# A two-layer hybrid trunk: the bias table loaded ready-made, transposes grouped, norm operations metered, boundary and last stage re-timed

## The chip, the cores and the metric

One core of one Trainium2 chip runs the whole kernel. The metric is device time in microseconds, the median of three runs. Its engines are TensorE (PE; PEld is its weight load), VectorE (DVE), ScalarE (ACT), GpSimd (POOL) and SyncE (SP), whose queue issues most DMA transfers.

## The reference

The input x is 256 x 2048 in float32. Each of two layers computes:

```
h    = rmsnorm(x, pre_g)
q,k,v,z_att,u,z_ssm = split(h @ w_in)            # 2048 x 6144
w    = softmax(q1 k1/8 + bias, mask) - lam * softmax(q2 k2/8 + bias, mask)   # 8 heads
att  = rmsnorm(w @ v, subln_g) * (1 - lam_init) * silu(z_att)
y    = Re(C h_state) + D u     # diagonal complex state space, 64 groups
ssm  = glu(gelu(y) @ w_glu) * silu(z_ssm)
x    = x + rmsnorm([att, ssm] @ w_out, post_g)
```

The bias is the T5 table: `table[bucket(key - query), head]`, the same for both layers. It depends on key minus query alone, so one row of 383 values per head says all of it.

## The kernel before

**Weights in two parts.** Every weight matrix is cut into half chunks of 128 x 1024, 288 in all (144 per layer). SP loads each into a `raw` tile, ScalarE rounds it to `hi` (`emit_hi`, L220), VectorE forms `lo` = raw - hi (`emit_lo`, L238). The activations have two parts as well (`hthi`, `htlo`). `main` (L1018) multiplies hi x hi, hi x lo and lo x hi, so a half chunk is 24 matmuls of 256 columns or 12 of 512. `emit_hi` and `emit_lo` run two half chunks ahead of `main`, SP six.

**Order within a layer** (half chunk numbers s): U4 and u, the state-space input (0 to 15), q and k (16 to 47), v and z_att (48 to 79), z_ssm (80 to 95), glu (96 to 111), out (112 to 143).

**Side work.** Everything else is written as generators, started by `hooks` (L1127) at a given s. In each half chunk `run_first` (L296) advances those that don't want TensorE, then come `emit_lo` and `main`, and `run_second` (L302) advances those that yielded a number, which is how many PSUM `side` buffers they want (four in all). So a `yield` is half a chunk's time. VectorE operations of long chains stand in two queues: `weave` (parameters, scan) and `urgent` (norms). `fill` (L206) takes from them before and after each `lo`, up to a budget in ns by the costs of `cost` (L126). The budget is a balance, `bal` (L1283), which gains 2880 ns (s < 48) or 2724 ns per half chunk, less `SPARE` and the work already issued. With `urgent` operations present the budget is `UB` = 1500 instead, and `fill` takes one from each queue in turn.

**Steps that the change touches.** `load_params` and `params_gen` (L319, L329) make the bias: a one-hot matrix times the table on TensorE (`psp`), a copy on ScalarE, a store to `tab`, a broadcast to `tabs`, and a load with a shifted address into `bias`. `rstd_gen` (L627) makes 1/rms of x; its last step is the matmul `psr` and the copy `rbc`, which the evacuations of U4 and u (`evac`, L950) need. `newton_ops` (L260) is an inverse square root by two steps. `prep_gen` (L470) clears `cm` on GpSimd and turns the state-space matrices into `wi` through transposes `psw`. `attfin_gen` (L932) scales and transposes one head of attention. `y_gen` (L795) makes the state-space output: matmuls `psy` and `psz`, GELU, transposes `psg`. At the boundary (L1229 to L1265) and at the end (L1295 to L1302) `rowend` (L1100) takes the norm of the out product for rows 0 to 127 (t = 0) and 128 to 255 (t = 1), `late_mg` (L1108) multiplies its last quarter by the norm weight, `add_ops` (L1112) adds x. `warm` (L1181) issues matmuls whose result nobody reads; `build` (L607) transposes x for the new layer (`psx`).

Of the kernel before, what the change touches and what calls it, by code (L numbers as in the profile page):

```python
# [39 lines left out]
W3 = 4  # L40
WB = 1
# [7 lines left out]
TPS = ([(0, 1024), (1024, 1024)], [(0, 512), (512, 768), (1280, 768)])  # L49
WY = 2  # L50
UB = 1500
# [35 lines left out]
def hybrid_trunk(ctx: ExitStack, tc, x, rel_bias, post_norm_g, xt_in, wst, vecs, poles, lams, bc, onehot, out):  # L87
# [57 lines left out]
    def mul(o, a, b):  # L145
        return tt(o, a, b, ALU.mult)
# [31 lines left out]
    tabs = dp.tile([128, 3072], F32, name="tabs")  # L178
    tab = dp.tile([8, 384], F32, name="tab")
# [26 lines left out]
    def fill(budget, force=False):  # L206
        while (budget > 0 and weave) or (urgent and (force or budget > 0)):
            if urgent:
                try:
                    budget -= next(urgent[0])  # L210
                except StopIteration:
                    urgent.popleft()
            if not weave or budget <= 0:
                continue
            try:
                budget -= next(weave[0])
            except StopIteration:
                weave.popleft()
# [19 lines left out]
    def emit_lo(hs, budget, halves=False, parts=(0, 1)):  # L238
# [6 lines left out]
        if (weave and budget > 0) or urgent:  # L245
            budget = UB if urgent else budget
# [13 lines left out]
    def newton_ops(o, v, n, i=0):  # L260
# [3 lines left out]
        yield ts(y.bitcast(I32), v.bitcast(I32), -0.5, float(0x5F380000), ALU.mult, ALU.add)  # L264
        yield mul(h, y, y)
# [53 lines left out]
    def load_params():  # L319
# [4 lines left out]
        G.dma_start(out=bt[0:32, 0:384], in_=onehot)  # L324
        G.dma_start(out=bt[0:32, 384:392], in_=rel_bias)
# [3 lines left out]
    def params_gen():  # L329
# [3 lines left out]
        yield 2  # L333
        ps = side("psp")
        mm4(ps[0:8, 0:320], bt[0:32, 384:392], bt[0:32, 0:320], True, True)
        ps2 = side("psp2")
        mm4(ps2[0:8, 0:64], bt[0:32, 384:392], bt[0:32, 320:384], True, True)
# [7 lines left out]
        act(bt[0:8, 1024:1344], ps[0:8, 0:320], AF.Copy)  # L345
        act(bt[0:8, 1344:1408], ps2[0:8, 0:64], AF.Copy)
        weave.append(params_ops(T, bt))
        SY.dma_start(out=tab, in_=bt[0:8, 1024:1408])
# [9 lines left out]
        SY.dma_start(out=tabs, in_=tab.rearrange("h r -> (h r)").unsqueeze(0).to_broadcast([128, 3072]))  # L358
        for _ in range(8):
            yield  # L360
        SY.dma_start(out=bias, in_=bass.AP(tensor=tabs.tensor, offset=tabs.offset + 127,
                                          ap=[[3071, 128], [384, 8], [1, 256]]))
# [107 lines left out]
    def prep_gen(l, slots):  # L470
# [55 lines left out]
        for b0 in range(0, 8, nb):  # L526
# [80 lines left out]
    def build(l, m):  # L607
# [19 lines left out]
    def rstd_gen(l):  # L627
# [43 lines left out]
        if l == 0:  # L671
            yield
# [46 lines left out]
    def s_gen(l):  # L719
# [6 lines left out]
        for b0 in range(0, 8, 2):  # L726
            if b0 == 4:
                while not (S["u2"] and f"wi{l}" in S):
                    yield
                yield  # L730
# [3 lines left out]
            for b in (b0, b0 + 1):  # L734
                wi = S[f"wi{l}" if b >= 4 else f"wa{l}"][b // 4]
                for h in range(2):
                    for a in range(2):
                        for r, g in ((0, 0), (1, 1), (1, 0), (0, 1)):
                            rows, o = slice(64 * g, 64 * g + 64), 64 * (g ^ r)
                            q, c = 2 * h + r, 256 * a + 64 * (2 * (b - b0) + h)  # L740
                            mm4(pss[r][o:o + 64, c:c + 64], wi[rows, b % 4, 2 * q + a], U[rows, 8 * q + b], True, True)
# [190 lines left out]
    def attfin_gen(l, h):  # L932
        yield from until(f"scal{l}{h // 4}")
        sc = S[f"scal{l}{h // 4}"]
        za = S["za"]
        for t in range(2):
            c = slice(1024 * t + 128 * h, 1024 * t + 128 * h + 128)
            act(za[:, c], za[:, c], AF.Copy, scale=sc[:, 2 * (h % 4) + t:2 * (h % 4) + t + 1])
# [3 lines left out]
        for t in range(2):  # L942
            tpose(ps[:, 128 * t:128 * t + 128], za[:, 1024 * t + 128 * h:1024 * t + 128 * h + 128], ident)
# [430 lines left out]
```

## Time and profile before

| | us |
|---|---|
| median of 3 runs (lowest, highest) | 923.97 (923.2, 924.18) |
| the profiled execution's own time | 924.31 |
| its span, first to last instruction | 922.5 |
| TensorE busy in the span | 901.3 |
| VectorE busy | 674.2 |
| ScalarE busy | 487.1 |
| GpSimd busy | 13.7 |

The mean granted TensorE clock is 0.99 of full speed. TensorE's busy time holds matmuls at either clock, and the matmuls of `warm`. A pause of any other engine costs time only if TensorE, or the end, waits for it.

### The profile page before, as it was taken

The numbers are of one execution on the slowest core, as the hardware profiler recorded it, in microseconds if no ns is written. First come the engines' busy times: TensorE is split into PE (matmuls) and PEld (weight loads), VectorE is DVE, ScalarE is ACT, GpSimd is POOL, SyncE is SP. The second block draws the span as 40 slices with busy tenths as digits, with TensorE's granted clock in tenths as the row PEclk, the third lists the DMA queues.
The fourth block names the chain that finished last, engine by engine and source line by source line (L and its number), as shares of the span: only waits on it lengthen the run. The fifth ranks groups of instructions, "written<-read, shape, count | busy, mean of one in ns | idle before, by whom it ended". The sixth has DMA issues, their size and how long they took to land.

```text
span 922.5 us, 16345 instructions
## 1 busy us (share of the span) xinstructions
PE 901.3 (98%) x6344; PEld 775.3 (84%) x6344; DVE 674.2 (73%) x1202; ACT 487.1 (53%) x878; POOL 13.7 (1%) x19
## 2 busy tenths in 40 slices
PE   9989999999999899999999999999999999999995
PEld 8989999888778688888889888887888888888884
DVE  5978894998975757898677549888966465665564
ACT  6623357465465576444469453445565665644451
POOL 2000000000000000000000000000000000000001
PEclk9999999999999999999999999999999999999998
DMA  8767566755452467567646765865545346665862
GB/s 326 233 190 233 182 218 170 224 176 166 138 183 94 136 224 233 172 226 242 211 152 188 247 209 130 267 198 168 178 137 182 116 138 205 203 208 165 293 181 92
DMA packets 65069, 176.11 MB, mean 191 GB/s; under 512 B 17574, under 2 KB 24512, under 8 KB 64096
## 3 DMA queue, kind: packets, MB, share of 16 engines
q1 hardware_dynamic: 64704, 174.89, 59.9%
q8 instruction: 50, 0.82, 0.4%
q14 instruction: 27, 0.22, 0.1%
q0 software_dynamic: 144, 0.15, 0.1%
q10 hardware_dynamic: 144, 0.03, 0.0%
HBM read 167.42 MB, written 7.88 MB: 190 GB/s over the span
## 4 chain that ended last, share of the span: by engine, by line
PE 86%; DVE 4%; ACT 2%; issue 1%; DVEq 0%; ACTq 0%
PE ac L139 78%; PE lga L139 1%; DVE lo L142 1%; PE psy L139 1%; PE po L139 1%; ACT wi L160 1%; PE pss L139 1%; DVE sct L142 1%; PE acu L139 1%; ACT hi L160 1%; PE pwt L123 1%; PE pst L139 0%; PE psm L123 0%; PE psf L123 0%; DVE nwh L142 0%
## 5 line engine op out<-in xcount | busy, mean ns | idle before, releaser
L160 ACT ACTIVATE hi<-raw 128x1024 fp32r<-128x1024 f32 (+1 forms) x282 | 298.1, 1057 | 358.8 <-PE ac L139 307.7
L142 DVE TENSOR_TENSOR lo<-raw,hi 128x1024 fp32r<-128x1024 f32 (+1 forms) x282 | 343.0, 1218 | 116.5 <-ACT hi L160 113.5
L139 PE MATMUL ac<-ht,hi 128*128 128x256 f32 (+1 forms) x1104 | 257.6, 319 | 3.7 <-DVE u L142 2.5
L139 PE MATMUL ac<-hi,ht 128*128 128x512 f32 x768 | 251.1, 398 | 0.0
L139 PEld LDWEIGHTS ac<-ht,hi 128*128 128x128 f32 x1104 | 184.3, 193 | 18.9 <-issue 2.9
L139 PE MATMUL ac<-ht,lo 128*128 128x256 f32 x704 | 199.3, 284 | 0.4 <-DVE lo L142 0.4
L139 PEld LDWEIGHTS ac<-hi,ht 128*128 128x128 f32 x768 | 144.9, 189 | 31.9
L139 PE MATMUL ac<-lo,ht 128*128 128x512 f32 x384 | 150.8, 393 | 2.1 <-DVE lo L142 2.0
L139 PE MATMUL ac<-hi,mx 128*128 128x512 f32 x456 | 141.8, 390 | 0.0
L139 PEld LDWEIGHTS ac<-ht,lo 128*128 128x128 f32 x704 | 135.2, 192 | 0.9 <-DVE lo L142 0.9
L139 PEld LDWEIGHTS ac<-hi,mx 128*128 128x128 f32 x456 | 85.6, 188 | 17.7
L139 PE MATMUL ac<-lo,mx 128*128 128x512 f32 x228 | 88.7, 389 | 0.0
L139 PEld LDWEIGHTS ac<-lo,ht 128*128 128x128 f32 x384 | 72.6, 189 | 17.5 <-DVE lo L142 3.7
L139 PE MATMUL ac<-hi,ghi 128*128 128x512 f32 x128 | 51.6, 403 | 0.0
L139 PEld LDWEIGHTS ac<-lo,mx 128*128 128x128 f32 x228 | 42.8, 188 | 8.9
L139 PE MATMUL ac<-hi,glo 128*128 128x512 f32 x128 | 50.2, 392 | 0.0
L139 PE MATMUL ac<-lo,ghi 128*128 128x512 f32 x128 | 49.9, 390 | 0.0
L149 DVE SCALAR_TENSOR_TENSOR y<-y 128x512 f32<-128x512 f32 x16 | 11.1, 692 | 28.2 <-ACT y L160 28.0
L160 ACT ACTIVATE att<-att,mx 128x128 f32<-128x128 f32 x64 | 28.4, 446 | 5.4 <-DVE mx L871 5.1
L139 PEld LDWEIGHTS ac<-hi,glo 128*128 128x128 f32 x128 | 24.0, 188 | 5.2
L139 PEld LDWEIGHTS ac<-lo,ghi 128*128 128x128 f32 x128 | 24.1, 188 | 4.6
L139 PEld LDWEIGHTS ac<-hi,ghi 128*128 128x128 f32 x128 | 24.0, 188 | 4.5
(202 smaller groups left out, 964.2 us busy)
## 6 DMA issues: line engine op xcount, KB each, us to landing
raw<-in_wst_dram SPq DMA_DIRECT2D x287, 512.0 KB, 4.0
U<-uds SPq DMA_DIRECT2D x48, 64.0 KB, 3.4
bt<-in_bc_dram SPq DMA_DIRECT2D x4, 512.0 KB, 6.4
uds<-u SPq DMA_DIRECT2D x4, 512.0 KB, 6.0
pg<-in_post_norm_g_dram SPq DMA_DIRECT2D x2, 1024.0 KB, 6.9
xt<-in_x_dram SPq DMA_DIRECT2D x2, 1024.0 KB, 7.4
xt<-xsave SPq DMA_DIRECT2D x2, 1024.0 KB, 6.2
tabs<-tab SPq DMA_DIRECT2D x1, 1536.0 KB, 8.3
```

Source lines behind the costliest of these rows:

```text
L123: P.transpose(o, i, idn)
L139: P.matmul(o, lhsT=l, rhs=r, start=start, stop=stop, skip_group_check=True)
L142: V.tensor_tensor(o, a, b, op=op)
L149: V.scalar_tensor_tensor(out=o, in0=a, scalar=s, in1=b, op0=op0, op1=op1)
L160: A.activation(out=o, in_=i, func=f, **kw)
```

## The change

- The bias comes as an input of 128 x 8 x 256, laid out on the host by copies of the table's entries, and is loaded in four pieces in halves 38 to 41. The one-hot product, `tab` and `tabs` are gone.
- `fill` takes `urgent` operations up to 330 ns per call first, charges them to the balance, and then takes from `weave`; `UB` is gone, `SPARE` for layer 0 from s = 44 is 100 instead of 200.
- `newton_ops` for one column merges two products into `scalar_tensor_tensor`.
- `rstd_gen(0)` has one `yield` less; u chunks of layer 0 are emptied after U4.
- The first chunk's products are issued product by product.
- Attention heads and gate parts are transposed two at a time; `wi` is copied in three instructions per block instead of four; in layer 0 the second half of the state input comes one `yield` earlier.
- `prep_gen(1)` starts at s = 102 instead of 96. At the boundary one more `psw` visit is issued, and the filler matmuls stand inside `build`.
- In the last stage the pieces for t = 1 are 768, 768, 512 columns, and the product with the norm weight runs on VectorE after the second.

```diff
-W3 = 4
-WB = 1
+W3 = 0
+WB = 2
+W5 = 6
-TPS = ([(0, 1024), (1024, 1024)], [(0, 512), (512, 768), (1280, 768)])
+TPS = ([(0, 1024), (1024, 1024)], [(0, 768), (768, 768), (1536, 512)])
-UB = 1500
...
-    def fill(budget, force=False):
-        while (budget > 0 and weave) or (urgent and (force or budget > 0)):
-            if urgent:
-                try:
-                    budget -= next(urgent[0])
-                except StopIteration:
-                    urgent.popleft()
-            if not weave or budget <= 0:
-                continue
+    def fill(budget):
+        left = 330.0
+        while urgent and left > 0:
+            try:
+                n = next(urgent[0])
+                left -= n
+                budget -= n
+            except StopIteration:
+                urgent.popleft()
+        while budget > 0 and weave:
...
-            budget = UB if urgent else budget
...
+        if n == 1:
+            w = st.tile([128, n], F32, tag=f"nww{i}", name="nww")
+            yield ts(w, v, 9.0 / 64.0, None, ALU.mult)
+            yield stt(h, y, y, v, ALU.mult, ALU.mult)
+            yield stt(h, h, -10.0 / 3.0, h, ALU.add, ALU.mult)
+            yield stt(y, h, 5.0, y, ALU.add, ALU.mult)
+            yield stt(h, y, y, w, ALU.mult, ALU.mult)
+            yield stt(o, h, -3.0, y, ALU.add, ALU.mult)
+            return
...
-        G.dma_start(out=bt[0:32, 0:384], in_=onehot)
-        G.dma_start(out=bt[0:32, 384:392], in_=rel_bias)
...
-        yield 2
-        ps = side("psp")
-        mm4(ps[0:8, 0:320], bt[0:32, 384:392], bt[0:32, 0:320], True, True)
...
-        act(bt[0:8, 1024:1344], ps[0:8, 0:320], AF.Copy)
...
-        SY.dma_start(out=tab, in_=bt[0:8, 1024:1408])
...
+        for h in range(0, HEADS, 2):
+            SY.dma_start(out=bias[:, h:h + 2], in_=bias_in[:, h:h + 2])
+            yield
...
-                for r in range(2):
-                    for g in range(2):
-                        act(wv[64 * g:64 * g + 64, :, r], psv[64 * r:64 * r + 64, :, :, g ^ r], AF.Copy)
+                act(wv[:, :, 0], psv[:, :, :, 0], AF.Copy)
+                for g in range(2):
+                    act(wv[64 * g:64 * g + 64, :, 1], psv[64 - 64 * g:128 - 64 * g, :, :, 1], AF.Copy)
...
+            if not m and not t:
+                warm(W5)
...
         yield from until(f"rst{l}")
-        if l == 0:
-            yield
         yield 1
         ps = side("psr")
...
-                yield
+                if l:
+                    yield
...
-        for t in range(2):
-            tpose(ps[:, 128 * t:128 * t + 128], za[:, 1024 * t + 128 * h:1024 * t + 128 * h + 128], ident)
+        for i in range(2):
+            for t in range(2):
+                c = 1024 * t + 128 * (h + i)
+                tpose(ps[:, 256 * i + 128 * t:256 * i + 128 * t + 128], za[:, c:c + 128], ident)
...
+            if l == 0 and seg == "u":
+                yield from until("u4")
...
-                for p in range(2):
-                    yield 1
-                    ps = side("psm")
+                yield 2
+                pss = [side("psm") for _ in range(2)]
+                for p, ps in enumerate(pss):
...
+                if l == 0 and b == 0 or part == 0:
+                    todo = [(kk, pr) for pr in ((0, 2, 1) if part is None else range(3)) for kk in ks]
+                else:
+                    todo = [(kk, None) for kk in ks]
...
-        if s == 96 and l + 1 < DEPTH:
+        if s == 102 and l + 1 < DEPTH:
             S["prep"] = prep_gen(l + 1, (8, (8, 2), (3, 4)))
...
-    SPARE = (150.0, 200.0, 300.0)
+    SPARE = (150.0, 100.0, 300.0)
...
                     rowend(1)
+                    for _ in range(2):
+                        advance(S["prep"])
...
-            late_mg(G, (t,))
-            for _ in add_ops(DEPTH - 1, t, TPS[t], True):
-                pass
+            if not t:
+                late_mg(G, (t,))
+            for n, _ in enumerate(add_ops(DEPTH - 1, t, TPS[t], True)):
+                if t and n == 1:
+                    late_mg(V, (t,))
```

## Rows read from the trace of the kernel before

**Rows 1.** The page: busy us (share of the span) x instructions of TensorE.

```profile
PE 901.3 (98%) x6344; PEld 775.3 (84%) x6344; DVE 674.2 (73%) x1202; ACT 487.1 (53%) x878; POOL 13.7 (1%) x19
```

**Rows 2.** Windows: length, then busy us (instructions) by engine, granted clock, DMA share, GB/s.

```profile
20.00:51.00 31.00, 30.87 (x256) 30.56 (x254) 28.35 (x86) 19.05 (x25) 0.00 (x0) 1.00 0.71 234
54.00:59.00 5.00, 5.00 (x31) 5.00 (x31) 2.27 (x5) 0.82 (x1) 0.00 (x0) 0.66 0.27 70
236.00:252.00 16.00, 14.74 (x63) 11.24 (x62) 16.00 (x23) 6.46 (x7) 0.00 (x0) 1.00 0.52 146
315.00:319.00 4.00, 4.00 (x12) 3.15 (x13) 3.75 (x6) 2.48 (x6) 0.00 (x0) 0.65 0.62 170
471.00:476.00 5.00, 4.86 (x26) 4.67 (x27) 3.62 (x7) 3.34 (x8) 0.00 (x0) 0.66 0.45 122
918.00:920.00 2.00, 0.00 (x0) 0.00 (x0) 0.86 (x1) 0.00 (x0) 0.00 (x0) 0.50 0.89 348
```

**Rows 3.** Timeline of the start: start us, us, engine, operation [idle before <-releaser].

```profile
11.45 0.38 PE L139 MATMUL ac<-ht,hi 128*128 128x256 f32 x1 [0.87 <-DVE ht L149]
...
17.27 0.81 PE L139 MATMUL psp<-bt 32*8 32x320 f32 x4
...
18.97 0.89 DVE L149 SCALAR_TENSOR_TENSOR ht<-xT,prm,ht 128x256 fp32r<-128x256 f32 x2 [1.82 <-ACT ht L160]
```

**Rows 4.** Timeline around the evacuation of U4 in layer 0.

```profile
51.36 0.38 ACT L160 ACTIVATE rbc<-psr 128x256 f32<-128x256 f32 x1 [2.37 <-PE psr L139]
...
51.78 1.48 DVE L142 TENSOR_TENSOR u<-acu,rbc 128x256 f32<-128x256 f32 x3 [1.02 <-ACT rbc L160]
53.11 1.98 DVE L142 TENSOR_TENSOR u<-ac,rbc 128x256 f32<-128x256 f32 x4
53.84 0.47 PE L139 MATMUL ac<-ht,hi 128*128 128x256 f32 x2 [2.51 <-DVE u L142]
```

**Rows 5.** Timeline of the third pause: VectorE, GpSimd and TensorE.

```profile
305.10 0.69 DVE L149 SCALAR_TENSOR_TENSOR y<-y 128x512 f32<-128x512 f32 x1 [3.25 <-ACT y L160]
...
308.02 1.85 DVE L154 TENSOR_SCALAR a<-a 128x8 f32<-128x8 f32 x1
...
308.04 1.81 POOL L475 MEMSET cm<- 128x2048 f32 x1 [143.38 <-PE psz L139]
...
313.01 0.63 PE L123 MATMUL psg<-ident,y 128*128 128x128 f32 x4 [2.15 <-DVE nwh L142]
...
314.74 0.79 PE L139 MATMUL ac<-lo,ht 128*128 128x512 f32 x1 [0.86 <-DVE lo L142]
```

**Rows 6.** Timeline of GpSimd's earlier memset and the VectorE operation beside it.

```profile
78.87 1.82 POOL L698 MEMSET t<- 128x2048 f32 x1 [73.33 <-DMA uds<-u]
...
79.60 1.23 DVE L142 TENSOR_TENSOR lo<-raw,hi 128x1024 fp32r<-128x1024 f32 x1
```

**Rows 7.** Timeline of the boundary between the layers.

```profile
467.31 1.06 PE L139 MATMUL warm<-ones 128*128 128x128 f32 x8
...
469.15 0.16 DVE L142 TENSOR_TENSOR nwh<-nwh,nv 128x1 f32<-128x1 f32 x1
469.34 0.16 DVE L149 SCALAR_TENSOR_TENSOR rs<-nwh,nwy 128x1 f32<-128x1 f32 x1
...
470.07 0.88 PE L123 MATMUL psx<-ident,xt 128*128 128x128 f32 x6 [1.48 <-DVE xt L149]
```

**Rows 8.** The chain that ended last, at one later visit: start us, us, what.

```profile
482.59 0.44 PE psw L123 x4
```

**Rows 9.** Timeline of the tail, and the group of `late_mg` on VectorE at the boundary.

```profile
913.97 1.26 POOL L1110 TENSOR_TENSOR mg<-mg,pg 128x512 f32<-128x512 f32 x1 [6.87 <-ACT mg L160]
914.01 1.24 DVE L142 TENSOR_TENSOR nwh<-nwh,nv 128x1 f32<-128x1 f32 x1
...
916.25 2.61 DVE L149 SCALAR_TENSOR_TENSOR xt<-mg,rs,xt 128x512 f32<-128x512 f32 x3
...
L1110 DVE TENSOR_TENSOR mg<-mg,pg 128x512 f32<-128x512 f32 x2 | 1.3, 684 | 0.0
```

More of the change, by code (lines that the diff above doesn't have):

```diff
@@ L86, in hybrid_trunk @@
 @with_exitstack
-def hybrid_trunk(ctx: ExitStack, tc, x, rel_bias, post_norm_g, xt_in, wst, vecs, poles, lams, bc, onehot, out):
+def hybrid_trunk(ctx: ExitStack, tc, x, post_norm_g, xt_in, wst, vecs, poles, lams, bc, bias_in, out):
     nc = tc.nc
@@ L740, in s_gen @@
                             q, c = 2 * h + r, 256 * a + 64 * (2 * (b - b0) + h)
-                            mm4(pss[r][o:o + 64, c:c + 64], wi[rows, b % 4, 2 * q + a], U[rows, 8 * q + b], True, True)
+                            mm4(pss[r][o:o + 64, c:c + 64], wi[rows, b % 4, 4 * h + 2 * (r ^ g) + a], U[rows, 8 * q + b], True, True)
             yield
@@ L941, in attfin_gen @@
         ps = side("psf")
-        for t in range(2):
-            tpose(ps[:, 128 * t:128 * t + 128], za[:, 1024 * t + 128 * h:1024 * t + 128 * h + 128], ident)
+        for i in range(2):
+            for t in range(2):
+                c = 1024 * t + 128 * (h + i)
+                tpose(ps[:, 256 * i + 128 * t:256 * i + 128 * t + 128], za[:, c:c + 128], ident)
         yield
-        act(S["mxhi"][:, h], ps[:, 0:256], AF.Copy, scale=subg[l])
-        stt(S["mxlo"][:, h], ps[:, 0:256], subg[l], S["mxhi"].bitcast(F32)[:, h], ALU.mult, ALU.subtract)
+        psv = ps.rearrange("p (i c) -> p i c", i=2)
+        act(S["mxhi"][:, h:h + 2], psv, AF.Copy, scale=subg[l])
+        stt(S["mxlo"][:, h:h + 2], psv, subg[l], S["mxhi"].bitcast(F32)[:, h:h + 2], ALU.mult, ALU.subtract)
         yield
@@ L963, in evac @@
                 mul(o, cut(a[:, 0:256]), cut(rbc))
+            if seg == "U4":
+                S["u4"] = True
         elif seg in ("q", "k"):
@@ L1000, in evac @@
                             tpose(ps[:, 256 * i + 128 * t:256 * i + 128 * t + 128], g[t][:, c:c + 128], ident)
+                yield
+                for p, ps in enumerate(pss):
                     k = 8 + 4 * n + 2 * p
@@ L1043, in main @@
             else:
-                for kk in range(2) if part is None else (part,):
-                    for pr in (None,) if part != 0 else range(3):
-                        for j in range(4):
-                            one(kk, j, pr)
+                ks = range(2) if part is None else (part,)
+                if l == 0 and b == 0 or part == 0:
+                    todo = [(kk, pr) for pr in ((0, 2, 1) if part is None else range(3)) for kk in ks]
+                else:
+                    todo = [(kk, None) for kk in ks]
+                for kk, pr in todo:
+                    for j in range(4):
+                        one(kk, j, pr)
             done = b == 3 and h == 1
@@ L1176, in hooks @@
                 at(cur[0], y_gen(l, j))
-        for h in range(8):
+        for h in range(0, 8, 2):
             if s == 96 + h:
@@ L1299, in hybrid_trunk, with _bucket, _lay @@
             rowend(t)
[L1300 to L1302 removed]
+            if not t:
[3 more added lines that the diff above has]
+                    late_mg(V, (t,))
         assert not gens and not weave and not starts, (gens, weave, starts)
[L1306 removed]
+_INS = ["x", "post_norm_g"]
 _OUTS = [((1, 256, 2048), "float32")]
[L1310 to L1320 removed]
+def _bucket(r):
+    rel = r - 255
+    n = abs(rel)
+    return max(i for i, s in enumerate(BUCKET_STARTS) if s <= n) + (16 if rel > 0 else 0)
+def _lay(np, x, rel_bias, pre_norm_g, w_in, w_glu, w_out, lambda_q1, lambda_k1, lambda_q2, lambda_k2, subln_g, ssm_a_re, ssm_a_im,
          ssm_log_dt, ssm_b_re, ssm_b_im, ssm_c_re, ssm_c_im, ssm_d, **rest):
@@ L1347, in _lay @@
     lay["bc"] = np.stack([pairs(a) for a in (ssm_b_re, ssm_b_im, *cs)], axis=2).reshape(2, 128, 2048)
-    lay["onehot"] = _onehot(np)
+    rows = rel_bias[[_bucket(r) for r in range(383)]].T
+    lay["bias"] = np.stack([rows[:, 127 - p:383 - p] for p in range(128)])
     return lay
```

26 lines of the change are left out of this document (4 added, 22 removed).

## The prediction

> **What bounds the kernel now.** I read the page's busy times first. TensorE is busy 98% of the span [rows 1], so the sum of matmul work is the floor, and the change can win only what lies on TensorE beside it: pauses, stretches at the lower clock, matmuls that needn't be there, and what comes after the last matmul. I then took the list of TensorE's waits and windows over the whole span with TensorE's busy time and the granted clock in them, and looked up each pause in the timeline. The reader is to see five places. (a) Near 11 us TensorE pauses 0.87 us for VectorE's second part of `ht` and then spends 0.81 us on the bias-table products `psp` [rows 3]. (b) Before 53.84 us it pauses 2.51 us, because the accumulators of U4 can't be emptied before `rbc` exists [rows 4]. (c) From 236 to 252 us VectorE is busy 16.00 of 16 us and TensorE 14.74 [rows 2]. (d) At 313 us it pauses 2.15 and 0.86 us [rows 5]. (e) At the layer boundary it pauses 1.48 us after eight filler matmuls [rows 7]. [...] Last, (f), a tail: VectorE's final additions start at 916.25, 3.5 us after the last matmul, and last 2.61 [rows 9].
>
> The profiled execution took 924.31 us, 1.81 outside its span of 922.5, and 0.34 more than the median of 923.97. I make the sum against 924.31 and take off 0.34 at the end.
>
> **The change, part by part.**
>
> *Start.* The bias table now arrives ready by four loads of 256 KB at half chunks 38 to 41, instead of matmuls, a 12 KB store, a 1.5 MB store and a 1 MB load. The `psp` products leave TensorE: 0.81 us [rows 3]. With them goes ScalarE's copy that stood in the queue ahead of the next `ht`, and so the 1.82 us that VectorE then waits [rows 3]; SP's store of the table, which held up the weight loads behind it, goes too. The first chunk's products are reordered (all products with `hthi` first, those with `htlo` last), so that the 0.87 us wait for `htlo` is covered by 16 other matmuls. Together 1.7 us at most. But TensorE then arrives earlier at halves 5 to 7, and from 20 to 51 us VectorE is busy 28.35 of 31 us [rows 2]; it keeps its own gain of up to 1.8 us, yet the parameter operations, handed out a half earlier, come in front. I take 1.3, between 0.8 (only `psp`) and 1.7.
>
> *`rbc` and U4.* The extra `yield` in `rstd_gen(0)` goes, so `psr` is issued after half 12 instead of 13. The hand-out of `urgent` operations also changes, from a budget of 1500 to 330 per call; by the costs at L147 the 14 operations take six calls of `fill` either way (the old one interleaved other operations), so the flag `rst0` comes in the same half. One half is worth about 2.88 us (L1283), more than the 2.51 us pause. In addition VectorE now empties U4 first; before, the three `acu` operations stood ahead of it from 51.78 to 53.11 [rows 4]. `psr` needs its `side` buffer beside three `acu` tiles: four in all, which fit. So the pause goes, and the stretch at clock 0.66 with it: 2.5 + 1.7 = 4.2. If only the order worked, it would be 1.3.
>
> *Scan.* While the operations of the head norm wait in `urgent`, the old `fill` ignores the balance and issues a large scan operation in each call: two of them and `lo` in one half, some 3.6 us of VectorE in a half of 2.72 (L1283). That is place (c), 1.26 us of pause. The new one charges the urgent operations to the balance. Against it stands `SPARE` 100 instead of 200 ns for halves from 44 on, about 35 halves and 3.5 us of scan work drawn earlier. I take 1.0 gain; the bounds are 1.3 gain and 1.0 loss.
>
> *Third pause.* VectorE is late at 313 us: its chain starts at 305.10 after a wait for ScalarE, runs ten norm operations around one `lo`, and one of these, the scaling of `a` by a constant, takes 1.85 us instead of 0.16, exactly while GpSimd's memset of `cm` runs [rows 5]. A memset at 78.87 did not slow the `lo` at 79.60, which took 1.23 us as elsewhere [rows 6]. So it is the kind of VectorE operation that meets it. [...]
> Moving `prep_gen` from half 96 to 102 does not move the memset: GpSimd waits in its queue for `psz`, not for program order [rows 5]. What moves is VectorE: with three urgent operations per call instead of five it has done the first two of its three constant-scaling steps by about 307.5 (305.10 + 0.6 + three steps of 0.2 + `lo`, 1.2) and the third only after `y`, and at 308.04 it is at the `zs` operations, which read PSUM. So 1.7 us come back, and about 0.6 more from five operations that move behind `lo`. The GELU result that released TensorE at 313.01 is there 2.3 earlier, before TensorE wants it: pause of 2.15 gone. `lo`, wanted 0.86 before 314.74, then comes about 0.5 after TensorE asks; I leave another 0.5 for the next halves. Gain 2.15 + 0.86 + 1.4 (clock) - 1.0 = 3.4; bounds 1.3 and 4.4.
>
> *Boundary.* Before, TensorE did 1.06 us of filler, then two transposes, then paused until VectorE's `xt` [rows 7]. Now the filler is 12 matmuls (8 took 1.06, so 1.6 us) between the two pairs of transposes, and one more `psw` visit of 0.44 us [rows 8] moves into the gap. The norm for one row has two dependent steps less; steps are 0.19 apart [rows 7], and I put a scalar read from memory at 0.05 each (an estimate), so 0.3. Of 1.06 + 1.48 - 0.3 = 2.2 us about 2.0 are now filled, so I expect the clock to stay up: 0.3 + 0.44 + 1.7 = 2.4. Without the clock 0.7.
>
> *Tail.* GpSimd's product of `mg` and `pg` at 913.97 holds VectorE's norm product for 1.24 us instead of 0.16 [rows 9]. It moves to VectorE, between the second and third addition, at 0.68 [rows 9]. Gain 1.08 + 0.3 (shorter norm) - 0.68 = 0.7. The last store is 256 instead of 384 KB; at the 348 GB/s of 918 to 920 us [rows 2] that is 0.37. I take 1.05, bounds 0.7 and 1.2.
>
> *At nothing:* the paired attention and gate transposes (the same number of transposes; TensorE waits for none of them before), the `wi` copies in three instead of four instructions, and `prep_gen` at 102, all covered by matmuls that run on; uncovered, a visit would cost its 0.44. In layer 1 three urgent operations per call make `psr` one half later; the accumulator that needs it is asked for a half after that, about 1.7 us of cover, without which up to 2.
>
> **Sum:** 1.3 + 4.2 + 1.0 + 3.4 + 2.4 + 1.05 = 13.35. 924.31 - 13.35 - 0.34 = 910.6 us.
>
> **Rivals.**
> 1. [...] Chance 0.13.
> 2. *`psr` is not earlier*: the flag comes a half later, and only the order of U4 helps. 910.6 + 2.9 = 913.5. Against it: the count of calls. Chance 0.09.
> 3. *VectorE becomes the bound of the scan*, the other side. At 236 to 252 us it has no reserve. If 100 ns less spare makes it late in every half from 44 to 80, the pauses recur and the clock goes to 0.65 as after 313 us; each us there costs 0.35, plus the pauses of 1.26 per 16 us. It decides at a stretch of some 30 us with both (10.5 + 2.4), which eats the 13; over 60 us it ends near 925 to 935. Against it: even with VectorE at 16.00 of 16 us in (c) the granted clock stayed at 1.00 [rows 2]. Chance 0.10, of which 0.04 within 0.2%.
> 4. *The pauses shrink, but the clock still falls at the three places*: 4.8 us back, 915.4. For it: some 0.5 us pauses remain. Chance 0.08.
>
> Forecast 0.60. Faster by over 0.2% (1.85 us, about what a measurement can tell): forecast, 1, 2 and 4, 0.90; within: 0.04; slower: 0.06. Low end: all upper bounds give 924.0 - 15.6, about 908.0 with rounding; high end past rival 4 by two weak terms, 917.5.
>
> **What would show it.** Right: no `psp`; `psr` before half 13; no TensorE wait over 0.5 us near 52 and no clock below 0.9 there; the scaling of `a` at 0.16 us; PE clock near 1.0 in the boundary; VectorE's last addition ends about 5.5 us after the last matmul instead of 6.2. Wrong: a new TensorE wait on `lo` in the scan, or on `rbc` in layer 1; a 1.8 us VectorE operation beside a GpSimd one; the stretches at 0.65 still there after shorter pauses.

## The result, and the profile after

The changed kernel takes 907.83 us (median of 4 runs, 906.83 to 908.64), against 923.76 for the kernel before on the same chip: ratio 0.9827, 95% interval 0.981 to 0.9844. The forecast was 910.6 with a range from 908.0, so the direction was right, but the time lies 0.2 us below the range's low end: the gain of 15.9 us was larger than the range allowed for. The profiled execution took 908.64, its span is 906.9.

The page after, first lines and the clock row of its 40 slices, answers to [rows 1]; TensorE's share rose to 99%. The clock row is the same as that of the kernel before. A slice is 23 us long and a 9 stands for 90% or more, so 5 us at 0.66 can't be seen in it; the windows further down show the clock:

```profile
span 906.9 us, 16284 instructions
...
PE 894.7 (99%) x6344; PEld 771.4 (85%) x6344; DVE 668.2 (74%) x1187; ACT 478.5 (53%) x852; POOL 11.4 (1%) x16
...
PEclk9999999999999999999999999999999999999998
```

Windows of the kernel after (length, busy us and instructions of PE, PEld, DVE, ACT, POOL, then granted clock, DMA share, GB/s), around U4, the scan, the third pause and the boundary; they answer to [rows 2]:

```profile
48.00:60.00 12.00, 12.00 (x103) 12.00 (x101) 11.15 (x31) 4.24 (x4) 0.00 (x0) 1.00 0.62 198
230.00:250.00 20.00, 20.00 (x93) 16.16 (x91) 18.74 (x37) 10.46 (x17) 0.00 (x0) 1.00 0.62 177
300.00:320.00 20.00, 19.54 (x89) 15.41 (x88) 15.41 (x26) 11.39 (x20) 0.63 (x1) 1.00 0.59 203
455.00:470.00 15.00, 14.51 (x121) 13.88 (x120) 13.06 (x30) 12.06 (x29) 0.00 (x0) 1.00 0.59 189
```

All of PE's waits that were named are gone or under 0.5 us, and the clock is 1.00 in each place. To see where the time went I followed the same instruction in both traces (the first `acu` product, the evacuations of `q`, `v`, the gates and the norms) and took the difference of its start times:

| up to | start before, after | earlier by | this stage | forecast |
|---|---|---|---|---|
| first `acu` product (half 8) | 33.02, 31.06 | 1.96 | 1.9 start | 1.3 |
| third q of layer 0 | 78.62, 72.44 | 6.18 | 4.2 `rbc`, U4 | 4.2 |
| v | 190.77, 183.92 | 6.85 | 0.7 | 0 |
| z_att | 266.85, 257.86 | 8.99 | 2.1 scan | 1.0 |
| z_ssm | 300.44, 291.22 | 9.22 | 0.2 | 0 |
| last z_ssm | 331.41, 318.43 | 12.98 | 3.8 third pause | 3.4 |
| out's last piece | 467.08, 453.84 | 13.24 | 0.3 | 0 |
| q of layer 1 | 534.50, 518.90 | 15.60 | 2.4 boundary | 2.4 |
| out of layer 1 | 912.72, 897.95 | 14.77 | -0.8 layer 1 | 0 |
| span's end | 922.5, 906.9 | 15.6 | 0.8 tail | 1.05 |

Timeline after, the places that answer to [rows 3 to 5]: start us, us, engine, operation [idle before <-releaser]. TensorE's wait for `ht` at the start is 0.43 and from ScalarE, `psr` comes at 45.90 in half 12, VectorE empties U4 (four `ac` tiles) at 46.94 and the three `acu` tiles after it without anybody waiting for it, and GpSimd's memset meets `zs`, while the scaling of `a` takes 0.18:

```profile
10.55 1.22 PE L139 MATMUL ac<-ht,hi 128*128 128x256 f32 x8 [0.43 <-ACT ht L160]
...
45.90 0.59 PE L139 MATMUL psr<-dg,ones 128*128 128x256 f32 x2
...
46.94 2.08 DVE L142 TENSOR_TENSOR u<-ac,rbc 128x256 f32<-128x256 f32 x4 [1.15 <-ACT rbc L160]
...
50.23 1.60 DVE L142 TENSOR_TENSOR u<-acu,rbc 128x256 f32<-128x256 f32 x3
...
298.59 1.28 DVE L149 SCALAR_TENSOR_TENSOR zs<-th,ac 128x512 f32<-128x512 f32 x2
298.82 1.81 POOL L471 MEMSET cm<- 128x2048 f32 x1 [161.62 <-PE psz L139]
...
301.48 0.18 DVE L154 TENSOR_SCALAR a<-a 128x8 f32<-128x8 f32 x1
...
302.97 0.50 PE L139 MATMUL ac<-lo,ht 128*128 128x512 f32 x1 [0.46 <-DVE lo L142]
```

Timeline after of the boundary and the tail, answering to [rows 7] and [rows 9]; the pause of 1.48 is 0.34, and the last addition ends at 903.47, 5.5 us after ScalarE takes up TensorE's last result at 897.95:

```profile
453.64 1.03 PE L123 MATMUL psw<-ident,z 128*128 128x128 f32 x8
454.73 1.50 PE L139 MATMUL warm<-ones 128*128 128x128 f32 x12
456.57 0.87 PE L123 MATMUL psx<-ident,xt 128*128 128x128 f32 x6 [0.34 <-DVE xt L149]
...
897.95 0.60 ACT L160 ACTIVATE junk<-ac 128x512 f32<-128x512 f32 x1 [6.98 <-PE ac L139]
...
902.01 0.68 DVE L1124 TENSOR_TENSOR mg<-mg,pg 128x512 f32<-128x512 f32 x1
902.72 0.75 DVE L149 SCALAR_TENSOR_TENSOR xt<-mg,rs,xt 128x512 f32<-128x512 f32 x1
```

One place more comes out of the same comparison. Before the first product of the state input (`pss`), TensorE of the kernel before waits 0.25 us for ScalarE, whose eight copies of `wi` last 3.13 us; in the changed kernel six copies last 2.34 and are done before `pss` is issued. Before, and after:

```profile
140.01 3.13 ACT L160 ACTIVATE wi<-psw 64x256 f32<-64x256 f32 x8
...
143.19 1.16 PE L139 MATMUL pss<-U,wi 64*64 64x64 f32 x62 [0.25 <-ACT wi L160]
```

```profile
132.77 2.34 ACT L160 ACTIVATE wi<-psw 128x256 f32<-128x256 f32 x6
...
136.43 1.16 PE L139 MATMUL pss<-U,wi 64*64 64x64 f32 x64
```

### The profile page after: what moved, and what is told of

The parts are those of the page before. It is cut to its first block, busy times and chain, and to the rows that moved or that the text cites. A ratio compares the mean times of both kernels' runs of the same rounds, so it can differ in the third digit from the quotient of the medians.

```text
span 906.9 us, 16284 instructions
## 1 busy us (share of the span) xinstructions
PE 894.7 (99%) x6344; PEld 771.4 (85%) x6344; DVE 668.2 (74%) x1187; ACT 478.5 (53%) x852; POOL 11.4 (1%) x16
## 4 chain that ended last, share of the span: by engine, by line
PE 95%; DVE 2%; ACT 1%; DMA 1%; issue 0%; SPq 0%; ACTq 0%; DVEq 0%
PE ac L139 84%; PE acu L139 3%; PE lga L139 1%; PE po L139 1%; PE psy L139 1%; PE pss L139 1%; DMA raw<-in_wst_dram 1%; PE psw L123 1%; PE pwt L123 1%; DVE lo L142 1%; DVE sct L142 0%; PE pst L139 0%; PE psm L123 0%; PE psf L123 0%; DVE xt L149 0%
## 5 line engine op out<-in xcount | busy, mean ns | idle before, releaser
L139 PE MATMUL ac<-ht,hi 128*128 128x256 f32 (+1 forms) x1104 | 253.7, 317 | 0.8 <-ACT ht L160 0.4
L139 PE MATMUL ac<-ht,lo 128*128 128x256 f32 x704 | 196.4, 282 | 0.4 <-DVE lo L142 0.4
L139 PEld LDWEIGHTS ac<-ht,hi 128*128 128x128 f32 x1104 | 180.8, 191 | 16.3 <-ACT ht L160 0.9
L139 PEld LDWEIGHTS ac<-ht,lo 128*128 128x128 f32 x704 | 133.1, 190 | 0.7 <-DVE lo L142 0.7
```

The source lines that it names most:

```text
L139: P.matmul(o, lhsT=l, rhs=r, start=start, stop=stop, skip_group_check=True)
```

## The experiments

Times are medians; ratios are to the kernel before on the same chip (the changed kernel's is 0.9827).

### The scan and the third pause

**Old hand-out in the changed kernel** (`a_oldfill`):

```diff
-    def fill(budget):            # 330 ns of urgent per call, then weave
+    def fill(budget, force=False):   # one from each queue in turn
...
+            budget = UB if urgent else budget      # UB = 1500
```

> The changed kernel (907.8 us) with the old hand-out of urgent operations alone put back: 1500 ns per half, one from each queue in turn. Theory, that the hand-out made the pauses of the scan and of the third place: the scan's four pauses return, 2.2 us counted from start to start of the matmuls, and the third pause with its stretch of low clock, 3.8 us: together about 6, so 912.5 to 914.5 us, with VectorE busy all the time near 225 to 245 us and a granted clock near 0.65 near 303 us. Rival, that SPARE or TensorE's earlier arrival made those gains: within 1 us of 907.8.

912.73 us, ratio 0.9876 (0.9859 to 0.9893). One half of it came: the third pause, 3.7 us by the trace. So the time lies in the expected range, though half of the reason given for it didn't come. The timeline of that kernel shows the mechanism again, the scaling by a constant held beside the memset, the one queued behind it late with it, and TensorE's two pauses:

```profile
298.39 1.85 DVE L155 TENSOR_SCALAR a<-a 128x8 f32<-128x8 f32 x1
298.50 1.74 DVE L150 SCALAR_TENSOR_TENSOR nwy<-nwh,nwy 128x8 f32<-128x8 f32 x1
...
298.41 1.81 POOL L472 MEMSET cm<- 128x2048 f32 x1 [161.78 <-PE psz L140]
...
303.38 0.63 PE L124 MATMUL psg<-ident,y 128*128 128x128 f32 x4 [2.14 <-DVE nwh L143]
305.10 0.80 PE L140 MATMUL ac<-lo,ht 128*128 128x512 f32 x1 [0.87 <-DVE lo L143]
```

The other half did not: no pause in the scan. My theory for the scan had fallen.

**`SPARE` 200 in the changed kernel** (`a_spare200`):

```diff
-    SPARE = (150.0, 100.0, 300.0)
+    SPARE = (150.0, 200.0, 300.0)
```

> The changed kernel with SPARE at 200 instead of 100 ns alone put back. Theory, that SPARE does nothing here because VectorE keeps a reserve once the hand-out is charged to the balance: 907 to 908.7 us and no new wait of TensorE. Rival, that SPARE carries part of the 2.2 us of the scan: 909 to 910 us with waits for lo near 225 to 245 us.

907.55, ratio 0.982 (0.9802 to 0.9838), and no pause in the scan: `SPARE` alone is worth nothing there. One wait moved: TensorE waits 0.87 us for `lo` at 295.47, where the changed kernel waits 0.46 at 302.97; the time doesn't show it.

**Old hand-out with the late state input, with the old `SPARE`, and with both** (`a_of_sgen`, `a_of_200`, `a_of_200_sgen`). The state input's edit, and in the second and third `SPARE` as above:

```diff
-                if l:
-                    yield
+                yield
```

> The changed kernel with the old hand-out of urgent operations and, as before, one yield more before the second half of layer 0's state input. With the old hand-out alone the pauses of 236 to 252 us did not come back, so my theory (the hand-out removed them) has fallen. New theory: they come back where the scan as a whole is one half chunk (2.9 us) later against TensorE, and that half came from this yield. Then this kernel shows pauses of lo near 230 to 250 us, start to start some 2 us, plus the third pause, and takes 912.7 + 2.2 + 0.6 = 915.5. Rival: the 100 ns of spare time per half removed them, over the 25 halves before; then no such pause here, and 912.7 to 913.3.

> The changed kernel with the old hand-out of urgent operations and SPARE 200 instead of 100 ns. Theory (the half chunk of the state input removed the scan's pauses): no pause of lo at 230 to 250 us, 912.7. Rival (the 100 ns per half did, drawing some 2.5 us of scan work ahead of the norm's operations): pauses as in the kernel before, about 2.2 us more than the old hand-out alone, 914.9.

> The changed kernel with the old hand-out, SPARE 200 and the yield before the second half of layer 0's state input, all as before. Whichever of the three removes the scan's pauses, they must be back here: waits on lo at 230 to 250 us, 2.2 us start to start; 912.7 + 2.2 + 0.6 = 915.5. If they are not back, the cause lies outside the scan's own settings (the earlier start of everything by 6 us, or the paired transposes), and the time is 912.7 to 913.3.

913.21, 911.94 and 914.25 us (ratios 0.989, 0.9873, 0.9898, each with some 0.002 either way). The times hardly separate, the traces do (913.21 is the time of the rival, the trace that of the theory). Both kernels with the late state input have pauses of 0.54 and 0.59, and of 0.57 and 0.54, for `lo` near 239 and 242 us, and their z_att comes 1.8 and 2.0 us later than with the old hand-out alone; the kernel with the old `SPARE` has none. So the late half chunk brings them back under the old hand-out, with either `SPARE`.

**Late state input with the new hand-out** (`a_sgen`, the state input's edit alone), and the reverse, **the new hand-out in the kernel before** (`b_fill`, `a_oldfill`'s diff turned round):

> The changed kernel with one yield more before the second half of layer 0's state input, as before; the hand-out of urgent operations stays new. Theory (the half chunk alone decides the scan's pauses): they come back at 225 to 242 us, 2.0 to 2.2 us start to start, 909.9. Rival (the new hand-out is enough by itself, and only the two old settings together bring them back): no pause, 907.5 to 908.2.

> The kernel before with the new hand-out of urgent operations alone. Theory for the third pause (the hand-out alone moves the three scalings by a constant off GpSimd's memset): no VectorE operation of 1.8 us beside it, pause of 2.15 gone, clock 1.00 there, 3.3 to 3.8 us gained. Theory for the scan (the half chunk of the state input removes its pauses): the pauses of 236 to 252 us stay; together 920.1 to 920.6. Rival (the hand-out removes the scan's pauses too, each of the two being enough): 2.2 us more, 918.0 to 918.4.

908.83 (ratio 0.9833, 0.9814 to 0.9852) with no pause in the scan, and 916.85 (0.9918, 0.9898 to 0.9938) with none there or at the third place. The rivals hold for the scan: each of the two edits is enough by itself. `b_fill` is 1.2 us faster than its rival said; in its profile the clock at the boundary is 1.00, where [rows 2] has 0.66, a difference of 1.4 us that its edit doesn't touch. One window of 20 us in four kernels shows it (PE's instructions are the first number in brackets). Before, and with the old hand-out and the late input in the changed kernel:

```profile
230.00:250.00 20.00, 18.74 (x84) 14.62 (x82) 19.93 (x31) 8.84 (x13) 0.00 (x0) 1.00 0.50 146
```

```profile
225.00:245.00 20.00, 18.87 (x83) 14.53 (x81) 19.83 (x32) 7.57 (x9) 0.00 (x0) 1.00 0.51 158
```

With the late input and the new hand-out, and with the early input and the old hand-out:

```profile
225.00:245.00 20.00, 20.00 (x94) 16.24 (x92) 18.31 (x34) 9.22 (x14) 0.00 (x0) 1.00 0.66 192
```

```profile
225.00:245.00 20.00, 20.00 (x93) 16.28 (x92) 19.37 (x37) 9.21 (x13) 0.00 (x0) 1.00 0.62 176
```

`b_fill` has `prep_gen` at half 96, `a_oldfill` at 102, and the third pause is gone in the first and there in the second: the move of `prep_gen` doesn't decide it, the hand-out does. But it does so in another way than in the changed kernel: in `b_fill` the memset runs at 313.89, and the last norm operation is over before 305, so that no constant-scaling step is near it at all:

```profile
304.03 0.17 DVE L142 TENSOR_TENSOR scal<-scal,rst 128x8 f32<-128x8 f32 x1
...
313.89 1.81 POOL L475 MEMSET cm<- 128x2048 f32 x1 [149.44 <-PE psz L139]
```

**A product instead of the scaling by a constant, in the kernel before** (`b_tt`):

```diff
-        yield ts(v, v, 9.0 / 64.0, None, ALU.mult)
+        if n == 8:
+            yield mul(v, v, c964)      # a tile that holds 9/64
+        else:
+            yield ts(v, v, 9.0 / 64.0, None, ALU.mult)
```

> The kernel before, with one edit: where the inverse square root works on 8 columns, the multiplication by the constant 9/64 becomes a product with a tile that holds 9/64, so an operation with two tensors in place of one tensor and a constant. Theory: the kind of operation decides whether it meets GpSimd's memset. Then the 1.85 us operation near 308 us takes some 0.16 to 0.2 beside the memset, VectorE is 1.7 us earlier, the pause of 2.15 us shrinks to about 0.5, and the kernel takes 921 to 922.5. Rival: whatever VectorE does beside that memset is held, the operation or its neighbour still takes 1.8 us, and the time stays at 924 to 925.

919.97 us, ratio 0.9954 (0.9939 to 0.997): about 4 us where I expected at most 3. The timeline of VectorE and GpSimd in that kernel: the product begins beside the memset and isn't held.

```profile
307.97 0.16 DVE L142 TENSOR_TENSOR a<-a,c 128x8 f32<-128x8 f32 x1
...
307.99 1.81 POOL L479 MEMSET cm<- 128x2048 f32 x1 [142.56 <-PE psz L139]
```

The pause shrinks from 2.2 to 0.6, and with it the low clock behind it goes (1.00 from 312 to 320 us): the stage gives 3.1. Another 1.8 us came at the boundary without any edit there, and 1.1 went in layer 1, also without one; the boundary's runs below and the last section bear on that. Beside the memset, which only writes, the scaling by a constant takes 1.85 us [rows 5] and the product of two tensors 0.16; beside the tail's GpSimd product, which reads `mg` and `pg`, a product of two tensors takes 1.24 [rows 9].

### `rbc` and U4

**`psr` a half later again** (`a_psr_late`), and **u emptied first again** (`a_u_first`):

```diff
         yield from until(f"rst{l}")
+        if l == 0:
+            yield
         yield 1
```

```diff
-            if l == 0 and seg == "u":
-                yield from until("u4")
```

> The changed kernel with the yield before psr in layer 0 put back alone; U4 is still emptied first. Theory, that both the earlier psr and the order were needed: a pause of about 1.2 us before half 14 (2.5 less the 1.3 of the three acu operations), and a stretch near clock 0.66 worth 1.4 to 1.7: 910.2 to 911 us. Rival, that the order alone suffices: under 908.7 us.

> The changed kernel without the wait that lets U4 be emptied before the u chunks. Theory, that psr one half earlier (2.88 us) covers even the old order, whose pause was 2.5 us: within 0.7 us of 907.8, no pause near 48 us. Rival, that the order is needed as well: 909 us or more, with a pause of 1.3 us.

910.07 (ratio 0.9843, 0.9825 to 0.9861) and 907.46 (0.9819, 0.9801 to 0.9837). With `psr` late TensorE pauses 1.12 us for `u`, as expected, but without the low clock that was expected behind it (1.00 from 50 to 56 us), and the trace is 1.4 us later from there on:

```profile
50.48 0.51 PE L139 MATMUL ac<-ht,hi 128*128 128x256 f32 x2 [1.12 <-DVE u L142]
```

With u first there is no pause at all. The half chunk decides; the order is a reserve that isn't drawn on.

### The start

**Bias by TensorE again** (`a_psp`: the changed kernel with `psp`, the copy, `tab`, `tabs` and the load put back), and **the first chunk's products in the old order** (`a_oldorder`):

```diff
-                if l == 0 and b == 0 or part == 0:
+                if part == 0:
```

> The changed kernel with the bias table made by TensorE again (one-hot product, copy, store, broadcast, load), everything else as changed. Theory (of the start's 1.9 us the products are 0.8 and the wait for the copy behind them some of the rest): 0.8 to 1.3 us lost by 35 us, 908.6 to 909.1. Rival 1 (the reordered first products alone bring the start's gain, and the store of the table is hidden): within 0.3 of 907.8. Rival 2 (with the next ht behind ScalarE's copy the new order loses too): 1.9 us lost, 909.7.

> The changed kernel with the first chunk's products in the old order, block by block. Theory (the order hides the 0.87 us that TensorE waited for the first htlo): 0.4 to 1.1 us lost by 35 us, 908.2 to 908.9. Rival (TensorE only waits later instead, for the next half's ht, so the order moves the wait): no loss, 907.8.

909.93 (ratio 0.9848, 0.983 to 0.9867) and 908.08 (0.9831, 0.9813 to 0.9849). The traces are 1.1 us later at q with `psp`, 0.3 with the old order, where the pause of 0.87 at 11.24 us is back. So most of the start's gain is the bias path; of the 1.9 us these two explain 1.4. The start itself differs from profile to profile: in the twelve other profiles with the start of the changed kernel the first `acu` product comes between 30.45 and 31.25 us (31.06 in the changed kernel's own), so a difference of 0.3 between two of them isn't resolved.

### The boundary

**Without the filler** (`a_nowarm`), and **the whole old boundary** (`a_boundary`), in the changed kernel:

```diff
-            if not m and not t:
-                warm(W5)
```

```diff
-W3 = 0
-WB = 2
-W5 = 6
+W3 = 4
+WB = 1
...
-                    for _ in range(2):
-                        advance(S["prep"])
```

> The changed kernel without the six filler visits (12 matmuls of 128 columns, whose result nobody reads) inside the transposes at the layer boundary. Theory (the filler keeps the clock at 1.00): TensorE then waits some 1.8 us for VectorE's xt at the boundary, the granted clock falls to about 0.66 for 5 us behind it, and the time rises by 1.5 to 1.9 us to 909.5. Rival (the clock of this place does not hang on the filler; in the kernel before with the changed scaling by 9/64 the same eight filler matmuls and the same pause of 1.49 us were followed by 1.00): the clock stays at 1.00 and the time stays at 907.8.

> The changed kernel with the boundary as before: eight filler matmuls ahead of the transposes instead of twelve between them, and one visit of state-space transposes instead of two there. Theory (my 2.4 us: 0.3 of norm, 0.44 of the visit and 1.7 of clock, of which the norm stays): a pause of about 1.4 us before the transposes of xt, clock 0.66 behind it, and 907.8 + 2.1 = 909.9. Rival (the fall of the clock there is a matter of the run, not of the filler): the pause, but clock 1.00 in the profiled execution, and 907.8 to 908.6.

907.93 (ratio 0.9835, 0.9815 to 0.9854) and 908.51 (0.9833, 0.9815 to 0.9851). TensorE pauses 1.68 and 1.22 us, and the clock stays up (mean 0.997 in both profiled executions, as in the changed kernel). Window behind the pause of 1.68 us, without the filler:

```profile
458.00:463.00 5.00, 5.00 (x44) 5.00 (x44) 3.77 (x9) 4.01 (x9) 0.00 (x0) 1.00 0.48 131
```

Both theories fell: the gain of clock at the boundary didn't hang on the filler in these runs. The times are those of the rivals.

**The new boundary alone in the kernel before** (`b_bound`, the two diffs above turned round):

> The kernel before with the new boundary alone: twelve filler matmuls between the transposes, two visits of state-space transposes there instead of one, and nothing else. Theory (as I put it: filler in place of the pause keeps the clock, 0.44 + 1.7): the pause of 1.48 us shrinks to about 0.6 and the stretch behind it keeps clock 1.00; 923.9 - 2.1 = 921.8. Rival (the fall of the clock at the boundary comes from what went before in the layer, the stretch after 313 us or the phase of the run; without the filler the changed kernel kept 1.00 there): 923.4 to 923.9, with the clock falling behind the filler in the same way.

922.55, ratio 0.9983 (0.997 to 0.9996), between the theory's time and the rival's. The pause is 0.60, the clock 1.00 behind it, and the trace gains 1.9 us there. But the same profile shows clock 1.00 from 54 to 59 us, behind the untouched pause of 2.5 us at U4, where the kernel before has 0.66, and a lower and longer stretch at the third pause than before:

```profile
54.00:59.00 5.00, 5.00 (x43) 5.00 (x43) 3.33 (x6) 1.06 (x1) 0.00 (x0) 1.00 0.34 75
...
312.00:320.00 8.00, 7.13 (x20) 5.48 (x19) 6.43 (x8) 4.83 (x10) 0.00 (x0) 0.57 0.52 141
```

**Old hand-out and old boundary together** (`a_of_boundary`, both diffs above), and **the kernel before once more** (`b_again`, no edit):

> The changed kernel with the old hand-out of urgent operations and the old boundary together. So far the clock fell at the boundary only in the kernel before, which has both a fall behind the pause near 313 us and the old boundary; each of the two alone left the boundary at 1.00. Theory (a fall at the third pause and the old boundary together are needed): the third pause and its low clock are back, and the clock falls behind the boundary's pause of 1.2 us too; 912.7 + 0.4 + 1.7 = 914.8. Rival (what follows a pause of 1.2 to 1.7 us differs from run to run, whatever came 150 us before): the boundary stays at 1.00 in the profiled execution, 913.1, and the timed runs spread over about 2 us.

> The kernel before, unchanged, profiled a second time. Theory (the kernel decides where the clock falls): the granted clock falls again behind all three pauses, to about 0.66 for 4 to 5 us, the boundary's among them. Rival (it differs from run to run): at one of the three, the boundary most likely, it stays at 1.00 or the low stretch is of another length by over 1 us. The time is 923 to 925 if all three fall, about 922 if the boundary doesn't.

910.6 (ratio 0.9865, 0.9843 to 0.9888) and 923.8 (1.0001, 0.9983 to 1.0018). In the first the clock does fall at the boundary in the profiled execution, to 0.71 from 460 to 465 us; that execution took 913.18 us, the three other runs 909.94 to 910.82. In the second, the very kernel of [rows 2] and with the same pause of 1.5 us, it doesn't:

```profile
54.00:59.00 5.00, 4.89 (x29) 4.92 (x30) 2.50 (x5) 0.44 (x1) 0.00 (x0) 0.67 0.31 60
...
315.00:319.00 4.00, 4.00 (x14) 3.21 (x15) 3.46 (x6) 3.22 (x6) 0.00 (x0) 0.78 0.46 151
...
471.00:476.00 5.00, 5.00 (x42) 5.00 (x43) 3.77 (x8) 4.36 (x10) 0.00 (x0) 1.00 0.49 113
```

That settles it for the rival: with this pause the same kernel keeps its clock in one run and loses it in another. It isn't so at each place: behind the third pause (2.15 us and a second wait after it) the clock fell in all 8 profiles that have it (0.65 in [rows 2], 0.57 and 0.78 above), and behind the 2.5 us at U4 in 4 of 5 (0.66 or 0.67). As to the times, 910.6 is 2.1 us less than the old hand-out alone took (912.73), although the kernel undoes more, so medians of four or five runs on different chips don't settle differences of that size here.

### The tail

**The last product on GpSimd again** (`a_tail_pool`):

```diff
-            if not t:
-                late_mg(G, (t,))
+            late_mg(G, (t,))
```

> The changed kernel with the last product of mg and the norm weight on GpSimd again, ahead of the additions; the pieces of 768, 768 and 512 columns stay. Theory (GpSimd's product holds VectorE's norm operation beside it, 1.08, against 0.68 for the product on VectorE): a norm product of some 1.2 us after the last matmul, the span's end 0.4 to 0.5 later after the last matmul, 908.2 to 908.3. Rival (GpSimd's product hits another operation or none): within 0.2 us of the changed kernel, or 0.7 faster as VectorE loses the product, 907.2.

908.16, ratio 0.9827 (0.9808 to 0.9845). GpSimd's product holds the norm operation beside it for 1.17 us instead of 0.16. From the norm's first operation to VectorE's end it is 0.3 us longer than in the changed kernel (897.45 to 902.54 against 898.67 to 903.47), and to the span's end 0.6; the medians differ by 0.3.

```profile
897.98 1.26 POOL L1124 TENSOR_TENSOR mg<-mg,pg 128x512 f32<-128x512 f32 x1 [6.86 <-ACT mg L160]
...
898.08 1.17 DVE L149 SCALAR_TENSOR_TENSOR nwh<-nwh 128x1 f32<-128x1 f32 x1
```

## Why the prediction was right and where it was wrong

**Start, 1.3 forecast, 1.9 in the trace.** The step failed in size. `psp` and what hangs on it cost 1.1 by the traces (2.1 by the medians), the order 0.3; my upper bound of 1.7 was too low. The remaining 0.5 I can't assign; starts of the same code differ by up to 0.8 between profiles.

**`rbc` and U4, 4.2 forecast, 4.2.** As worked out: `psr` in half 12, no pause, clock 1.00. That the order alone would give 1.3 was too little: with `psr` late, 4.2 - 1.4 = 2.8 of it remained in the trace, because behind the pause of 1.12 us the clock stayed up in that profile.

**Scan, 1.0 forecast, 2.1.** This is the step with the largest error: it went 0.8 us past its own upper bound of 1.3, where the time lies 0.2 us out of the range. It failed twice. In size: "that is place (c), 1.26 us of pause" took the idle time that the trace shows for the whole loss, and made 1.3 the bound. The shown idle begins only at the end of a matmul, and matmuls overlap: one of 512 columns lasts 0.39 us while the next starts 0.23 after it. Counted in starts, the 20 us of 230 to 250 hold 84 instructions before and 93 after [windows above]; nine at 0.23 are 2.1 us. In cause: charging the urgent operations was enough by itself (`b_fill`, `a_sgen`), as forecast, but so was the half chunk by which the state input comes earlier, which I had costed at nothing (`a_oldfill`). `SPARE`, from which I feared 1.0 of loss, did nothing. VectorE's busy time in that window fell from 19.93 to 18.74.

**Third pause, 3.4 forecast, 3.8.** The mechanism is shown, down to the place: at the memset VectorE is at `zs`, which takes 1.28 us beside it (that it would not be held was my estimate), and the last scaling comes after `y`. `b_tt` shows that the kind of operation is what matters (0.16 against 1.85 us), `a_oldfill` that the hand-out is what shifts it; in `b_fill` it parts memset and norm altogether, by 9.7 us. The surplus is that one leftover of 0.46 us came where I had left 1.0.

**Boundary, 2.4 forecast, 2.4, for a reason that doesn't hold.** I made it of 0.3 and 0.44 for steps and a visit taken off, and 1.7 for the clock. The first two terms came about as said. The first product of layer 1 is 0.26 us earlier in every kernel with the shorter norm, in `a_boundary` too, and not in `b_bound`; and near 500 us, where one visit fewer is left to do, kernels with the new boundary gain 0.4 (`b_bound`) to 0.7 us (the changed kernel), those with the old one 0.0 to 0.3. (The 0.05 for a scalar from memory was my estimate and came from no row; the tail after shows 0.06: such a norm step takes 0.22 us, the others 0.16.) The clock is the third term: by the trace the kernel before without a fall there (`b_again`) gains 1.4 by itself. (`a_boundary`, which keeps the norm, is only 0.1 later there by its trace, 0.7 by its median; a few tenths aren't resolved.) The three terms for the clock, 1.7 at U4, 1.4 at the third pause and 1.7 here, were my estimate, (1 - granted clock) x length of the windows in [rows 2]. No run shows one of them by itself; where the boundary's fall stayed away without an edit there, the traces gained 1.4 (`b_again`) and 1.8 us (`b_tt`). The 1.7 for the clock here was "filled, so the clock stays up". That is the step that failed: without the filler the clock stays up too in the profiled execution, and the kernel before has it at 0.66 in one profile and at 1.00 in another. So it was luck that the forecast's 2.4 was met: it met a difference that the profile before happened to show. Over all profiles: with the old boundary or without the filler, behind pauses of 1.2 to 1.7 us, the clock fell in 2 of 7 (to 0.66 and 0.71); with the new boundary, behind pauses of at most 0.6 us, in none of 13. The filler may therefore be worth something on the mean (one of five runs without it took 910.07 at mean clock 0.995, the others 907.4 to 908.7 at 0.996 or 0.997), but no run here shows more than that.

**Tail, 1.05 forecast, 0.8.** The held operation went as said, and the distance from the last matmul is the forecast 5.5 us.

**At nothing.** Between q and v of layer 0 another 0.7 us was gained that I had not costed. By the matmul starts it is 0.65, all of it at the first state-input products, in all 15 profiles with the changed kernel's `wi` copies, whichever other edit was taken back in them, and at most 0.05 in the five of the kernel before and its variants. The lines above show why: TensorE waited for the last of eight `wi` copies, and three copies per block instead of four end that wait. So putting the copies at nothing, as covered, was wrong; that is by elimination, since no run takes the copies back alone. Another 0.2 to 0.3 us per layer comes at glu in the same 15 profiles, where the paired transposes stand; which of the edits there gives it wasn't tested. `psr` of layer 1 is later, and nothing waits for it, as forecast. Layer 1 lost 0.8, on which below.

**Sum.** Start 0.6, scan 1.1, third pause 0.4, the stretches costed at nothing 0.7 + 0.2 + 0.3, less 0.8 in layer 1 and 0.25 in the tail: some 2.2 us of the 2.8 by which the forecast was high. The other 0.5 is between executions: the profiled one is 0.8 above its median, where I had allowed 0.34 for the one before. The low end was also summed wrongly: the upper bounds as stated, 1.7, 4.2, 1.3, 4.4, 2.4 and 1.2, make 15.2 and not 15.6, and 924.0 - 15.6 is 908.4. Bounds on the scan and the `wi` copies of the size that they showed (2.1 and 0.65) would have covered the result. None of the rivals came: no VectorE operation was held beside the memset, `psr` was earlier, the scan has more reserve, and the clock didn't fall.

No version beat the changed kernel by more than the measurement: 907.46 with u first and 907.55 with `SPARE` 200 lie inside its 906.83 to 908.64.

## What to carry to other kernels

Where matmuls overlap (here they last 0.39 us and start every 0.23), count the instructions in two windows of equal length; the idle time shown before a late one is only what is left after the modelled end of the one ahead. A VectorE operation of 0.17 us that took 1.85 beside GpSimd's memset cost over three microseconds here, because its results gate TensorE: changing its kind (a product with a tile for a scaling by a constant) brought 3.1 us, moving it 3.8. In the tail operations with two inputs took 1.24 [rows 9] and 1.17 us (`a_tail_pool`) instead of 0.16 beside a GpSimd product that reads, so a change to that kind would not have helped there. A wait of 0.25 us on the list is worth following too: this one stood for 0.65. Before a low clock behind a pause is booked as a gain, profile the kernel a second time: here two profiles of one kernel gave 0.66 and 1.00.

## What was not expected of the hardware

**The fall of the clock differs from run to run.** The same code and the same pause of 1.5 us gave a granted clock of 0.66 from 471 to 476 us in one profile of the kernel before [rows 2] and 1.00 in the other (`b_again`). What decides it no run shows. Of the 57 timed runs of the kernel before that stood beside the experiments, the four with a mean clock of 0.995 took 920.85 us on the mean, the 17 with 0.992 took 924.41.

**In layer 1 the same matmuls ran at two paces.** The changed kernel and the one with the GpSimd tail are the same up to 898 us and have clock 1.00, yet between about 550 and 608 us the first falls behind by 1.1 us. In the first trace a pair of a 512-column and a 256-column product starts every (592.01 - 589.89) / 6 = 0.353 us, in the second every (592.15 - 589.72) / 7 = 0.347:

```profile
589.89 0.40 PE L139 MATMUL ac<-ht,hi 128*128 128x512 f32 x1
590.13 0.28 PE L139 MATMUL ac<-ht,lo 128*128 128x256 f32 x1
...
592.01 0.40 PE L139 MATMUL ac<-ht,hi 128*128 128x512 f32 x1
```

```profile
589.72 0.39 PE L139 MATMUL ac<-ht,hi 128*128 128x512 f32 x1
589.95 0.28 PE L139 MATMUL ac<-ht,lo 128*128 128x256 f32 x1
...
592.15 0.39 PE L139 MATMUL ac<-ht,hi 128*128 128x512 f32 x1
```

No idle time is shown in either. This is the loss of layer 1 in the changed kernel's profile (1.1, less the 0.3 gained at glu). The slow pace through that stretch shows in 11 of the 20 profiles, `b_tt` and `b_fill` among them, and not in `before`, `b_again`, `a_u_first` or `a_oldorder`, so it belongs to the run, not to the change; what sets the pace was not found.
